# Gated DeltaNet heads 4 to 7: output made channel by token, its norm summed with products with ones

## Chip, cores and metric

The kernel runs on one core of one Trainium2 chip. The time is the device time of one execution in microseconds (us); for the kernel before it is the median of three runs.

## What is computed

One layer of a decoder: RMSNorm of x (1024 tokens of 2048 channels), one projection into three head groups, a gate on each, one output projection, a residual sum and a last RMSNorm. The change touches group B, the gated delta rule: 8 heads, 128 channels for keys and for values. Cut to what matters:

```python
q = l2norm(to_heads(q)) * DN_HEAD_DIM ** -0.5        # l2norm: x * rsqrt(sum(x*x) + EPS)
k = l2norm(to_heads(k)); v = to_heads(v)
...                                                   # per chunk, state S (128 x 128) of a head:
v_new = val_c - kcd_c @ S
o_c = qg_c @ S + ai_c @ v_new                         # qg = q * exp(g_cum), ai = tril(q k^T * decay)
S = S * exp(g_last) + kd_c.T @ v_new
...
o = rmsnorm(o, dn_norm_g) * silu(d_z)                 # o * rsqrt(mean(o*o) + EPS) * g, per token and head
```

The output o is linear in q. So the kernel runs the recurrence with q not normed, and puts the norm of q into that of o: with q not normed, o is scaled by rsqrt(mean(o*o) + 128 * EPS * sum(q*q) + 128 * EPS * EPS).

## The kernel before

All work is in fp32. The large products (projection, memory keys and values, output projection) split each operand into a high and a low fp32r part and add three products (`triple`, L574). The two large projections run as seven products of half-size blocks each (`seven`, L1340). Their weights come from HBM through the `raw` and `kept` tiles and are split by ScalarE (a cast into `rhi`) and VectorE (the rest into `rlo`); the left sides go the same way into `lh` and `ll` or `lm`. `split_to` (L564) is this pair of instructions.

Tokens are worked in two halves `hf` of 512 (HT), each of four tiles of 128 (NT = 4, P = 128). Heads go in pairs `p` of two, and heads 0 to 3 (h < NJ = 4) before heads 4 to 7. For a pair and a half there are two parts:

- `front` (L1230) takes q and k of each head, channel by token: a causal convolution with Silu (`conv`, L978), then `qk` (L1000). `qk` turns k to token by channel with four transposes into one PSUM bank (`to_tokens`, L971), sums its squares by token (`sumsq`, L996: four ScalarE passes, each with a read of its accumulator) and scales it into `kd` (`by_token`, L992: four ScalarE passes with a scale per token). It turns q in the same way, sums its squares into `hs[:, 0]`, forms the products of k with k and with q, and multiplies q by the row of decays exp(g_cum), loaded for all partitions from `ecs[hf]` (L1014, L1035). The tiles q, k, `kd` and `ai` go to HBM (`late_d`, L1240), and the two small columns that are needed later go to `late_hs`.
- `back_of` (L1647) calls `front_late` (L1247), which loads the four tiles into `qT`, `kT`, `kd` and `ai` and copies the small columns back into `hs`; `load_u`, for the inverse of the chunk matrix; `values` (L1261), for v; and `back` (L1268), which makes four steps of the recurrence, `scan_step` (L1170), and then `heads_out` (L1211).

A scan step has four groups of products of 128 by 128 per head. The last, L1199 to L1202, makes the output with q and `ai` as standing operands, so that it comes out token by channel. `S.copy(vs, d0)` (L1209) takes it out of PSUM.

`heads_out` sums the squares of the output by token, forms the factor with a power on POOL (`rsqrt_to`, L559), scales the output by token, and turns it with four transposes to channel by token. For heads 0 to 3 ScalarE scales it by the norm's weights (`col2[:, 8:9]`) and it is stored. For heads 4 to 7 the gate, which lies in `g_d`, is loaded into a tile `E` and one VectorE instruction multiplies by weights and gate (L1227); `head_done` (L1675) stores the result.

**Order of the work.** Nothing is issued while the program is written: every call makes an `Op` in a `Plan`. `issue` (L402) lays all operations on the engines with a price for each (`price`, L193; a VectorE pass of n columns is (n + 151) / 0.96 ns, L223), takes deadlines from a pass backwards (`late`, L342), moves the deadlines named in the table `SHIFT` (L75, operation number and ns) and lays the work once more. Each engine, SyncE's queue of DMA issues included, then runs its operations strictly in that order. TensorE's order is thereby fixed too: groups of small products are laid between the large ones. `FITS` (L41) names the ScalarE functions that need a table of their own.

**Tiles.** `ring["kT"]`, `qT`, `vs`, `kd` and `ai` are two slots each; a new tile in a slot waits for every user of the old one (`Slots`, L475). In the backs `front_late` uses the same two sets of five tiles (`back_sets`, L1635) each time. After the last back the slots hold the queries of group C (`cqs`, L1811). `own_set` is four tiles that the fronts use.

Of the kernel before, what the change touches and what calls it, by code (L numbers as in the profile page):

```python
# [11 lines left out]
F32R = mybir.dt.float32r  # L12
AF = mybir.ActivationFunctionType
# [5 lines left out]
P = 128  # L19
# [18 lines left out]
KP = 4  # L38
ON_ACT = (3,)
NEG = -1.0e30  # L40
FITS = {AF.Exp: 1, AF.Silu: 2, AF.Gelu_apprx_tanh: 3}  # L41

# [21 lines left out]
class Plan:  # L64
# [8 lines left out]
    FETCH = 3500.0  # L73
    TABLE, HOLD = 1300.0, 6000.0
    SHIFT = {  # L75
# [5 lines left out]
    }  # L81

    def __init__(self, nc):
# [340 lines left out]
def kernel(  # L424
# [101 lines left out]
    ring["E"] = Ring("E", 2, [P, HT])  # L526
    ring["tn"] = Ring("tn", 4, [P, HT])
    ring["xr"] = Ring("xr", 3, [P, HT + 3])
    ring["hs"] = Ring("hs", 4, [P, 10, NT])
    jk = C([P, HT], "jk", mybir.dt.bfloat16)  # L530
    gr = C([NT * NH, P], "gr")
    small = Ring("small", 8, [P, 8])
# [8 lines left out]
    def tpb():  # L541
# [9 lines left out]
    G.affine_select(out=ident, in_=ident, compare_op=ALU.not_equal, fill=1.0, base=0,  # L551
                    pattern=[[-1, P]], channel_multiplier=1)
    G.memset(ones, 1.0)
    mhalf = C([P, 8], "mhalf")
    G.memset(mhalf, -0.5)
    with rank(0):
# [443 lines left out]
    def qk(h, hf, tiles, hs, gt, bank):  # L1000

        q, k = tiles[:2]
        kd, ai, vs = map(tok, (*tiles[2:4], ring["tn"]()))
        beta, edk = (scs[hf][:, i] for i in (0, 4))
        (kt,) = to_tokens((k, bank))
        sumsq(hs[:, 1], kt)
        V.tensor_scalar(hs[:, 1], hs[:, 1], EPS, None, op0=ALU.add)
        V.reciprocal(hs[:, 3], hs[:, 1])
        V.scalar_tensor_tensor(hs[:, 2], hs[:, 3], -1.0, beta[:, :, h], op0=ALU.mult, op1=ALU.mult)
        V.tensor_tensor(out=hs[:, 3], in0=hs[:, 2], in1=edk[:, :, h], op=ALU.mult)  # L1010
        by_token(kd, kt, hs[:, 3])
        e = tok(ring["E"]())
        Q.dma_start(e.rearrange("p t c -> p (t c)"), e_d[hf][h])
        Q.dma_start(vs.rearrange("p t c -> p (t c)"), row_of(ecs[hf], h))  # L1014
        by_token(e, e, hs[:, 2])
        (qt,) = to_tokens((q, bank))
        sumsq(hs[:, 0], qt)
        V.tensor_scalar(hs[:, 0], hs[:, 0], P * EPS, P * EPS * EPS, op0=ALU.mult, op1=ALU.add)
        rsqrt_to(hs[:, 4], hs[:, 1])
        V.tensor_tensor(out=hs[:, 4], in0=hs[:, 4], in1=hs[:, 1], op=ALU.mult)  # L1020

        ch, cl = (ring["inv"](F32R).rearrange("p (t s c) -> p t s c", s=2, c=P) for _ in range(2))
        for i, src in enumerate((k, q)):
            split_to(ch[:, :, i], cl[:, :, i], tok(src), V)
        for t2 in range(NT // 2):
            d = bank
            for j in range(2):
                tt = 2 * t2 + j
                triple(d[:, j * 2 * P : (j + 1) * 2 * P], (ch[:, tt, 0], cl[:, tt, 0]), (ch[:, tt], cl[:, tt]),
                       True, True, R.cls)  # L1030
            dv = d.rearrange("p (t s c) -> p t s c", s=2, c=P)
            ts = slice(2 * t2, 2 * t2 + 2)
            V.tensor_tensor(out=gt[:, ts], in0=dv[:, :, 0], in1=e[:, ts], op=ALU.mult)
            V.tensor_tensor(out=ai[:, ts], in0=dv[:, :, 1], in1=e[:, ts], op=ALU.mult)
        V.tensor_tensor(out=q, in0=q, in1=vs.rearrange("p t c -> p (t c)"), op=ALU.mult)  # L1035

    def blocks_out(gt, n):

# [131 lines left out]
    def scan_step(hf, hp, tt, qs, ks, rest, ut):  # L1170

        egl, ngb = scs[hf][:, 3], scs[hf][:, 5]
        sl = slice(tt * P, (tt + 1) * P)
        heads = []
        for i, h in enumerate(hp):
            kd, ai, vs = (t[:, tt] for t in rest[i])
            at = 2 * i if scan_banks[0] is scan_banks[1] else 0
            d = [scan_banks[i][:, (at + k) * P : (at + k + 1) * P] for k in range(2)]
            heads.append((st[h], qs[i][:, sl], ks[i][:, sl], kd, ai, vs, ut[:, i, tt], *d, r3[i], ww[i],
                          egl[:, tt, h : h + 1], ngb[:, tt, h : h + 1]))  # L1180

        first, last = hf == tt == 0, (hf, tt) == (1, NT - 1)
        with rank(1):
            if not first:
                with R.together():
                    for s, q, k, kd, ai, vs, u, d0, d1, r, w, e, n in heads:
                        PE.matmul(d0, k, s, start=True, stop=True)
                for s, q, k, kd, ai, vs, u, d0, d1, r, w, e, n in heads:
                    V.scalar_tensor_tensor(r, d0, n, vs, op0=ALU.mult, op1=ALU.add)
            with R.together():  # L1190
                for s, q, k, kd, ai, vs, u, d0, d1, r, w, e, n in heads:
                    PE.matmul(d1, u, vs if first else r, start=True, stop=True)
            for s, q, k, kd, ai, vs, u, d0, d1, r, w, e, n in heads:
                S.activation(w, d1, AF.Copy, scale=-1.0)
            with R.together():
                if not last:
                    for s, q, k, kd, ai, vs, u, d0, d1, r, w, e, n in heads:
                        PE.matmul(d1, kd, w, start=True, stop=True)
                for s, q, k, kd, ai, vs, u, d0, d1, r, w, e, n in heads:  # L1199
                    if not first:  # L1200
                        PE.matmul(d0, q, s, start=True, stop=False)
                    PE.matmul(d0, ai, w, start=first, stop=True)  # L1202
            for s, q, k, kd, ai, vs, u, d0, d1, r, w, e, n in heads:
                if first:
                    V.tensor_copy(s, d1)
                elif not last:
                    V.scalar_tensor_tensor(s, s, e, d1, op0=ALU.mult, op1=ALU.add)
            for s, q, k, kd, ai, vs, u, d0, d1, r, w, e, n in heads:
                S.copy(vs, d0)  # L1209

    def heads_out(hf, hp, hss, rest):  # L1211
        obs = [vs for kd, ai, vs in rest]

        for hs, ob in zip(hss, obs):
            sumsq(hs[:, 5], ob)
            V.scalar_tensor_tensor(hs[:, 6], hs[:, 5], 1.0 / P, hs[:, 0], op0=ALU.mult, op1=ALU.add)
            rsqrt_to(hs[:, 7], hs[:, 6])
            by_token(ob, ob, hs[:, 7])
        for h, ob, bank in zip(hp, obs, scan_banks):
            (tp,) = to_tokens((ob.rearrange("p t c -> p (t c)"), bank))  # L1220
            if h < NJ:
                S.activation(ob, tp, AF.Copy, scale=col2[:, 8:9])
                Q.dma_start(tok(o_d[hf][h]), ob)
            else:
                e, y = ring["E"](), ob.rearrange("p t c -> p (t c)")
                Q.dma_start(e, g_d[hf][h - NJ])
                V.scalar_tensor_tensor(ob, tp, col2[:, 8:9], tok(e), op0=ALU.mult, op1=ALU.mult)  # L1227
                head_done(h, hf, y)

    def front(p, hf, banks):  # L1230

# [2 lines left out]
        for i, h in enumerate(hp):  # L1234
# [1 line left out]
            conv(1, h, hf, tiles[1])  # L1236
            conv(0, h, hf, tiles[0])
            qk(h, hf, tiles, hs, gt[:, i], banks[i])
            V.tensor_copy(late_hs[:, hf, h], hs[:, 0:5:4])
            for d, t in zip(late_d[hf][h], tiles[:4]):  # L1240
                Q.dma_start(d, t)
        gdr = blocks_out(gt, f"{hf}{p}")
# [4 lines left out]
    def front_late(p, hf):  # L1247

        hp = (2 * p, 2 * p + 1)
        qs, ks, hss, rest = [], [], [], []  # L1250
        for h, tiles in zip(hp, back_sets):
            hss.append(ring["hs"]())
            V.tensor_copy(hss[-1][:, 0:5:4], late_hs[:, hf, h])
            for d, t in zip(late_d[hf][h], tiles):
                Q.dma_start(t, d)
            qs.append(tiles[0])
            ks.append(tiles[1])
            rest.append([tok(t) for t in tiles[2:]])
        return hf, hp, qs, ks, hss, rest

    def values(hf, hp, qs, ks, hss, rest):  # L1261
        for i, h in enumerate(hp):
            v = ring["tn"]()
            conv(2, h, hf, v)
            bank = scan_banks[i]
            by_token(rest[i][2], to_tokens((v, bank))[0], hss[i][:, 4])

    def back(hf, hp, qs, ks, hss, rest, ut):  # L1268
        for tt in range(NT):
            scan_step(hf, hp, tt, qs, ks, rest, ut)  # L1270
        heads_out(hf, hp, hss, rest)


    late_hs = C([P, 2, NH, 2, NT], "lhs")

    def halves(t):
        n = t.shape[1] // 2
# [476 lines left out]
    scan_banks = dnr.bufs[0:2]  # L1754
    hand = dnr.bufs[3]
    wide = acc
    el = over([abh[:, 0:HT], ring["tn"].bufs.pop()])
    for hf in range(2):
        spatial(hf)
# [331 lines left out]
```

## Time and profile before

| | |
|---|---|
| median of 3 runs | 1561.24 us (1560.71 to 1561.47) |
| profiled execution | 1558.44 us |
| its span, first to last instruction | 1556.7 us |
| granted TensorE clock, mean | 0.998 |
| HBM read and written | 336.58 MB, 100.40 MB |
| fronts of heads 4 to 7 | within 600 to 850 us of the span |
| recurrences of heads 4 to 7 | within 965 to 1175 us |

How to read the lines below: an engine is PE (TensorE), PEld (its weight loads), DVE (VectorE), ACT (ScalarE), POOL (GpSimd) or SP (SyncE, which only issues DMA). A group has the form "line engine operation out<-in shape xcount | busy us, mean ns of one | idle time of the engine before them, and what ended it". Since all operations are issued at L420, groups are told apart by tile names, with the buffer number left out: `dn` and `acc` are PSUM banks, `os` is a tile of `own_set`, and a transpose is a product with `ident`, so `dn<-ident,vs` turns a `vs` tile. A product of two full fp32 tiles shows as four records (x112 is 28 products), a transpose or an fp32r product as one. Records of products overlap: their pace is the distance of their starts. A row of a stretch gives start and end, length, busy time and number of instructions by engine, then granted clock, DMA share and GB/s. A row of waits is "who <- for whom: us in total, times, longest".

### The profile page before, as it was taken

The numbers are of one execution on the slowest core, as the hardware profiler recorded it, in microseconds if no ns is written. First come the engines' busy times: TensorE is split into PE (matmuls) and PEld (weight loads), VectorE is DVE, ScalarE is ACT, GpSimd is POOL, SyncE is SP. The second block draws the span as 40 slices with busy tenths as digits, with TensorE's granted clock in tenths as the row PEclk, the third lists the DMA queues.
The fourth block names the chain that finished last, engine by engine and source line by source line (L and its number), as shares of the span: only waits on it lengthen the run. The fifth ranks groups of instructions, "written<-read, shape, count | busy, mean of one in ns | idle before, by whom it ended". The sixth has DMA issues, their size and how long they took to land.

```text
span 1556.7 us, 25174 instructions
## 1 busy us (share of the span) xinstructions
PE 1546.4 (99%) x8725; PEld 1299.2 (83%) x8725; DVE 1250.4 (80%) x1843; ACT 947.8 (61%) x1942; POOL 102.0 (7%) x125
## 2 busy tenths in 40 slices
PE   9999999999999999999999999999999999999997
PEld 8988888888888888888888888888888888888886
DVE  6966974777898946788789975878758999998996
ACT  7833385565874335698885454776557874464554
POOL 0100000100021000010111010010000000000000
PEclk9999999999999999999999999999999999999999
DMA  9999976999879797786797987999958999775984
GB/s 326 308 303 332 310 258 220 308 329 311 297 248 296 239 276 223 265 281 198 260 327 270 326 242 230 310 328 333 346 208 271 314 333 328 268 254 198 342 276 174
DMA packets 348642, 438.68 MB, mean 282 GB/s; under 512 B 78553, under 2 KB 183394, under 8 KB 348514
## 3 DMA queue, kind: packets, MB, share of 16 engines
q1 hardware_dynamic: 346930, 434.37, 85.4%
q0 software_dynamic: 1088, 2.10, 0.5%
q8 instruction: 69, 1.13, 0.3%
q10 hardware_dynamic: 496, 0.61, 0.1%
q14 instruction: 59, 0.48, 0.1%
HBM read 336.58 MB, written 100.40 MB: 281 GB/s over the span
## 4 chain that ended last, share of the span: by engine, by line
PE 95%; DVE 3%; issue 1%; ACT 1%; DMA 0%; POOL 0%; POOLq 0%; SPq 0%; DVEq 0%; ACTq 0%
PE acc L420 60%; PE dn L420 35%; DVE rlo L420 1%; DVE ll L420 0%; DVE tn L420 0%; DVE obs L420 0%; DVE raw L420 0%; DVE inv L420 0%; DMA raw<-in_w_mem_kv_dram 0%; ACT E L420 0%; DVE rs L420 0%; DVE kept L420 0%; DVE xa L420 0%; ACT lh L420 0%; DVE small L420 0%
## 5 line engine op out<-in xcount | busy, mean ns | idle before, releaser
L420 PE MATMUL acc<-lh,rhi 128*128 128x512 f32 x1024 | 395.4, 395 | 0.0
L420 PE MATMUL acc<-lh,rlo 128*128 128x512 f32 x1024 | 384.8, 396 | 0.0
L420 ACT CAST rhi<-raw 128x1024 fp32r<-128x1024 f32 (+1 forms) x145 | 183.3, 1265 | 210.1 <-PE dn L420 106.6
L420 DVE TENSOR_TENSOR rlo<-raw,rhi 128x1024 fp32r<-128x1024 f32 (+1 forms) x145 | 215.5, 1486 | 95.8 <-ACT rhi L420 83.7
L420 PE MATMUL acc<-ll,rhi 128*128 128x512 f32 x688 | 267.1, 395 | 0.1
L420 PEld LDWEIGHTS acc<-lh,rhi 128*128 128x128 f32 x1024 | 192.3, 188 | 37.0 <-ACT qT L420 0.2
L420 PEld LDWEIGHTS acc<-lh,rlo 128*128 128x128 f32 x1024 | 191.6, 188 | 37.0
L420 PEld LDWEIGHTS acc<-ll,rhi 128*128 128x128 f32 x688 | 129.2, 188 | 25.1 <-DVE ll L420 0.6
L420 DVE TENSOR_TENSOR ll<-ll,lh 128x1024 fp32r<-128x1024 f32 x105 | 128.3, 1222 | 11.0 <-ACT lh L420 10.3
L420 PE MATMUL acc<-lm,rhi 128*128 128x512 f32 x336 | 131.6, 394 | 0.0
L420 ACT CAST lh<-ll 128x1024 fp32r<-128x1024 f32 (+1 forms) x107 | 111.5, 1043 | 23.8 <-PE dn L420 9.7
L420 PE MATMUL dn<-lh,rhi 128*128 128x512 f32 x288 | 112.6, 393 | 0.0
L420 PE MATMUL dn<-lh,rlo 128*128 128x512 f32 x288 | 110.8, 394 | 0.0
L420 PE MATMUL dn<-ll,rhi 128*128 128x512 f32 x192 | 75.1, 392 | 0.0
L420 DVE TENSOR_TENSOR rlo<-kept,rhi 128x1024 fp32r<-128x1024 f32 (+1 forms) x38 | 52.7, 1389 | 25.6 <-ACT rhi L420 25.5
L420 PEld LDWEIGHTS acc<-lm,rhi 128*128 128x128 f32 x336 | 63.2, 188 | 12.0
L420 ACT CAST rhi<-kept 128x1024 fp32r<-128x1024 f32 (+1 forms) x38 | 45.3, 1192 | 42.7 <-PE acc L420 25.4
L420 DVE TENSOR_TENSOR raw<-raw,kept 128x1536 f32<-128x1536 f32 (+1 forms) x42 | 64.3, 1532 | 3.2 <-DMA raw<-in_w_in_dram 2.3
L420 POOL TENSOR_TENSOR hs<-hs,mhalf 128x4 f32<-128x4 f32 x32 | 45.8, 1433 | 298.1 <-DVE hs L420 298.1
L420 PEld LDWEIGHTS dn<-lh,rhi 128*128 128x128 f32 x288 | 54.2, 188 | 10.2
L420 PEld LDWEIGHTS dn<-lh,rlo 128*128 128x128 f32 x288 | 54.1, 188 | 10.4
L420 POOL TENSOR_TENSOR small<-small,mhalf 128x1 f32<-128x1 f32 x26 | 19.7, 758 | 634.4 <-DVE small L420 634.4
(500 smaller groups left out, 3460.1 us busy)
## 6 DMA issues: line engine op xcount, KB each, us to landing
raw<-in_w_in_dram SPq DMA_DIRECT2D x168, 256.0 KB
raw<-in_w_in_dram SPq DMA_DIRECT2D x72, 512.0 KB
raw<-in_w_out_dram SPq DMA_DIRECT2D x64, 512.0 KB
ll<-hsd SPq DMA_DIRECT2D x54, 512.0 KB
lm<-hsd SPq DMA_DIRECT2D x26, 512.0 KB
pd<-obs SPq DMA_DIRECT2D x48, 256.0 KB
late<-os SPq DMA_DIRECT2D x44, 256.0 KB
ll<-h0d SPq DMA_DIRECT2D x18, 512.0 KB
```

Of the source, the lines that this page charges most:

```text
L420: o.fn(*o.args, **o.kw)
```

## The change

For heads 4 to 7 the last two products of a scan step have their operands exchanged, so that the output comes out channel by token; it is not turned afterwards. The norm then needs sums over partitions, one for each token: `heads_out` forms (in place of q and k) 128 * EPS * q*q + o*o / 128 + EPS * EPS for each channel and token, splits it, and multiplies it by a matrix of ones, `ones_r`, which puts the sum over all channels into every partition. The factor is the square root of the reciprocal of that sum. q is no longer turned or summed in `qk`, and it is stored without the decay row; `front_late` loads the row into one of two tiles `faded` (from `own_set`) and multiplies there, so that the plain q stays in `qT`. For heads 0 to 3 the old way stands under the name `heads_turned`, with the small columns in `late_hs` and `late_q`. `front_late` takes new tiles from the slots for every pair; the high and low parts of the split are new tiles in the slots of `kd` and `ai`. `Sqrt` becomes a fourth function with a table of its own in `FITS`. The table of deadlines is another one: 30 entries in place of 33, for the operations as they are now numbered.

```diff
-FITS = {AF.Exp: 1, AF.Silu: 2, AF.Gelu_apprx_tanh: 3}
+FITS = {AF.Exp: 1, AF.Silu: 2, AF.Gelu_apprx_tanh: 3, AF.Sqrt: 4}
...
-        410: 8000, 616: -3000, 5881: 8000, 6077: -25600, 6106: 10700, 6120: -9300, 6123: -4300, 6178: 11600,
...
+        5947: -23300, 5980: 8700, 5990: -8000, 5994: -8000, 6011: 11300, 7734: 8000, 8595: -8000, 8727: 23300,
...
+    ones_r = C([P, P], "onesr", F32R)
+    with rank(0):
+        S.copy(ones_r, ones)
...
     def qk(h, hf, tiles, hs, gt, bank):
...
-        Q.dma_start(vs.rearrange("p t c -> p (t c)"), row_of(ecs[hf], h))
+        if h < NJ:
+            Q.dma_start(vs.rearrange("p t c -> p (t c)"), row_of(ecs[hf], h))
         by_token(e, e, hs[:, 2])
-        (qt,) = to_tokens((q, bank))
-        sumsq(hs[:, 0], qt)
-        V.tensor_scalar(hs[:, 0], hs[:, 0], P * EPS, P * EPS * EPS, op0=ALU.mult, op1=ALU.add)
+        if h < NJ:
+            (qt,) = to_tokens((q, bank))
+            sumsq(hs[:, 0], qt)
+            V.tensor_scalar(hs[:, 0], hs[:, 0], P * EPS, P * EPS * EPS, op0=ALU.mult, op1=ALU.add)
...
-        V.tensor_tensor(out=q, in0=q, in1=vs.rearrange("p t c -> p (t c)"), op=ALU.mult)
+        if h < NJ:
+            V.tensor_tensor(out=q, in0=q, in1=vs.rearrange("p t c -> p (t c)"), op=ALU.mult)
...
     def scan_step(hf, hp, tt, qs, ks, rest, ut):
...
-                for s, q, k, kd, ai, vs, u, d0, d1, r, w, e, n in heads:
-                    if not first:
-                        PE.matmul(d0, q, s, start=True, stop=False)
-                    PE.matmul(d0, ai, w, start=first, stop=True)
+                for s, q, k, kd, ai, vs, u, d0, d1, r, w, *_ in heads:
+                    for n, pair in enumerate(((q, s), (ai, w))[first:]):
+                        PE.matmul(d0, *(pair if hp[0] < NJ else reversed(pair)), start=n == 0, stop=n + first == 1)
...
+    def heads_out(hf, hp, raw_q, ks, rest):
+
+        for h, q, k, (kd, ai, vs), bank in zip(hp, raw_q, ks, rest, scan_banks):
+            o, e = vs.rearrange("p t c -> p (t c)"), ring["E"]()
+            S.activation(q, q, AF.Square, scale=math.sqrt(P * EPS))
+            S.activation(k, o, AF.Square, scale=1.0 / math.sqrt(P))
+            V.scalar_tensor_tensor(q, k, EPS * EPS, q, op0=ALU.add, op1=ALU.add)
+            hi, lo = ring["kd"](F32R), ring["ai"](F32R)
+            split_to(hi, lo, q, V)
+            with R.together():
+                PE.matmul(bank, ones_r, hi, start=True, stop=False)
+                PE.matmul(bank, ones_r, lo, start=False, stop=True)
+            V.reciprocal(k, bank)
+            S.activation(k, k, AF.Sqrt)
+            V.tensor_tensor(out=o, in0=o, in1=k, op=ALU.mult)
+            Q.dma_start(e, g_d[hf][h - NJ])
+            V.scalar_tensor_tensor(o, o, col2[:, 8:9], e, op0=ALU.mult, op1=ALU.mult)
+            head_done(h, hf, o)
...
     def front_late(p, hf):
...
+        for h in hp:
+            tiles = [ring[tag]() for tag in ("qT", "kT", "kd", "ai", "vs")]
             for d, t in zip(late_d[hf][h], tiles):
                 Q.dma_start(t, d)
-            qs.append(tiles[0])
+            q = tiles[0]
+            if h >= NJ:
+                q = faded()
+                Q.dma_start(q, row_of(ecs[hf], h))
+                V.tensor_tensor(out=q, in0=q, in1=tiles[0], op=ALU.mult)
+            raw_q.append(tiles[0])
+            qs.append(q)
...
+    faded = over(own_set[0:2])
```

More of the change, by code (lines that the diff above doesn't have):

```diff
@@ L528 @@
     ring["xr"] = Ring("xr", 3, [P, HT + 3])
-    ring["hs"] = Ring("hs", 4, [P, 10, NT])
+    ring["hs"] = Ring("hs", 4, [P, 5, NT])
     jk = C([P, HT], "jk", mybir.dt.bfloat16)
@@ L1002, in qk @@
         q, k = tiles[:2]
-        kd, ai, vs = map(tok, (*tiles[2:4], ring["tn"]()))
+        kd, ai = map(tok, tiles[2:4])
+        vs = tok(ring["tn"]()) if h < NJ else None
         beta, edk = (scs[hf][:, i] for i in (0, 4))
@@ L1209, in scan_step, with heads_turned @@
                 S.copy(vs, d0)
[L1211 to L1218, printed above, removed]
+    def heads_turned(hf, hp, rest):
+        obs, hss = [vs for kd, ai, vs in rest], [ring["hs"]() for _ in hp]
+        for h, hs, ob in zip(hp, hss, obs):
+            sumsq(hs[:, 1], ob)
+            V.scalar_tensor_tensor(hs[:, 2], hs[:, 1], 1.0 / P, late_q[:, hf, h], op0=ALU.mult, op1=ALU.add)
+            rsqrt_to(hs[:, 3], hs[:, 2])
+            by_token(ob, ob, hs[:, 3])
@@ L1219, in heads_out @@
         for h, ob, bank in zip(hp, obs, scan_banks):
             (tp,) = to_tokens((ob.rearrange("p t c -> p (t c)"), bank))
[L1221 to L1228, printed above, removed]
+            S.activation(ob, tp, AF.Copy, scale=col2[:, 8:9])
@@ new lines, in heads_turned @@
+            Q.dma_start(tok(o_d[hf][h]), ob)
+    def heads_out(hf, hp, raw_q, ks, rest):
[15 more added lines that the diff above has]
+            head_done(h, hf, o)
@@ L1238, in front @@
             qk(h, hf, tiles, hs, gt[:, i], banks[i])
-            V.tensor_copy(late_hs[:, hf, h], hs[:, 0:5:4])
+            V.tensor_copy(late_hs[:, hf, h], hs[:, 4])
+            if h < NJ:
+                V.tensor_copy(late_q[:, hf, h], hs[:, 0])
             for d, t in zip(late_d[hf][h], tiles[:4]):
@@ L1249, in front_late, with values @@
         hp = (2 * p, 2 * p + 1)
[L1250 to L1253, printed above, removed]
+        qs, ks, raw_q, rest = [], [], [], []
+        for h in hp:
+            tiles = [ring[tag]() for tag in ("qT", "kT", "kd", "ai", "vs")]
             for d, t in zip(late_d[hf][h], tiles):
                 Q.dma_start(t, d)
-            qs.append(tiles[0])
+            q = tiles[0]
[5 more added lines that the diff above has]
+            qs.append(q)
             ks.append(tiles[1])
             rest.append([tok(t) for t in tiles[2:]])
-        return hf, hp, qs, ks, hss, rest
-    def values(hf, hp, qs, ks, hss, rest):
+        return hf, hp, qs, ks, raw_q, rest
+    def values(hf, hp, qs, ks, raw_q, rest):
         for i, h in enumerate(hp):
@@ L1265, in values, with back @@
             bank = scan_banks[i]
-            by_token(rest[i][2], to_tokens((v, bank))[0], hss[i][:, 4])
-    def back(hf, hp, qs, ks, hss, rest, ut):
+            by_token(rest[i][2], to_tokens((v, bank))[0], late_hs[:, hf, h])
+    def back(hf, hp, qs, ks, raw_q, rest, ut):
         for tt in range(NT):
             scan_step(hf, hp, tt, qs, ks, rest, ut)
-        heads_out(hf, hp, hss, rest)
-    late_hs = C([P, 2, NH, 2, NT], "lhs")
+        if hp[0] < NJ:
+            heads_turned(hf, hp, rest)
+        else:
+            heads_out(hf, hp, raw_q, ks, rest)
+    late_hs, late_q = C([P, 2, NH, NT], "lhs"), C([P, 2, NJ, NT], "lhq")
     def halves(t):
```

7 rows, old and new, of the table SHIFT are left out of this document.

## Prediction

> **What bounds the kernel now.** I read the page first: busy time by engine, then the chain that ended last.
>
> ```profile
> span 1556.7 us, 25174 instructions
> ...
> PE 1546.4 (99%) x8725; PEld 1299.2 (83%) x8725; DVE 1250.4 (80%) x1843; ACT 947.8 (61%) x1942; POOL 102.0 (7%) x125
> ...
> PE 95%; DVE 3%; issue 1%; ACT 1%; DMA 0%; POOL 0%; POOLq 0%; SPq 0%; DVEq 0%; ACTq 0%
> ```
>
> TensorE is busy 99% of the span and is 95% of the chain. A busy PE row can hide stalls, so the next view was the list of waits, for TensorE alone; these two rows are all it has:
>
> ```profile
> PE acc L420 <- POOL ones L420: 1.2, 1, 1.2
> PE dn L420 <- ACT lh L420: 0.2, 1, 0.2
> ```
>
> TensorE waits 1.4 us in 1556.7. So the time is the number of TensorE instructions times the pace of each, and every other engine matters only if it makes TensorE wait. The pace of the large products stands in the chain in order of time, and that of a transpose group in the timeline of TensorE:
>
> ```profile
> 855.26 23.58 PE acc L420 x104
> ```
>
> ```profile
> 1016.87 0.39 PE L420 MATMUL acc<-lh,rhi 128*128 128x512 f32 x1
> 1017.10 0.60 PE L420 MATMUL dn<-ident,tn 128*128 128x128 f32 x4
> 1017.45 0.71 PE L420 MATMUL acc<-lh,rhi 128*128 128x512 f32 x2
> 1018.00 0.60 PE L420 MATMUL dn<-ident,vs 128*128 128x128 f32 x4
> ```
>
> 104 products of 512 columns take 23.58 us, 0.227 us each (the 0.39 us of a row is one product's latency, which overlaps the next). From 1016.87 to 1018.00 lie three such products and one group of four transposes: 1.13 - 3 x 0.227 = 0.45 us for the group. A group of four transposes costs TensorE as much as two products of 512 columns.
>
> **The change, part by part.** *TensorE.* For heads 4 to 7 and both halves of the sequence, eight cases, the change removes the group that turns q in `qk` and the group that turns the output in `heads_out`. The rows by group, the first in the stretch 600 to 850 us, where the fronts of heads 4 to 7 run, the other three in 1000 to 1175 us, where their recurrences run:
>
> ```profile
> L420 PE MATMUL dn<-ident,os 128*128 128x128 f32 x64 | 9.6, 272 | 0.0
> ```
>
> ```profile
> L420 PE MATMUL dn<-steps,ai 128*128 128x128 f32 x56 | 10.7, 275 | 0.0
> L420 PE MATMUL dn<-states,qT 128*128 128x128 f32 x52 | 10.0, 275 | 0.0
> ...
> L420 PE MATMUL dn<-ident,vs 128*128 128x128 f32 x32 | 4.6, 272 | 0.0
> ```
>
> The 64 `os` records are 16 groups, of which the eight of q go (those of k stay); the 32 `vs` records are the eight output groups, and all go. Removed: 16 x 0.45 = 7.2 us. Added: two products of 512 columns with ones per case, 16 x 0.227 = 3.6 us. The two output products of each scan step only swap which operand stands still; all are 128 by 128 either way and both rows show 275 ns, so that is 0. Net on TensorE: 7.2 - 3.6 = 3.6 us less, one transpose group's worth per case.
>
> *VectorE, where the recurrences run.* The busy time by stretch, from the first recurrence step of heads 4 and 5 to past the last of heads 6 and 7, and as a comparison a stretch of the output projection:
>
> ```profile
> core 0: us, PE busy (x) PEld busy (x) DVE busy (x) ACT busy (x) POOL busy (x), PEclk, DMA share, GB/s
> 965.00:1010.00 45.00, 45.00 (x309) 38.59 (x308) 36.17 (x52) 31.61 (x64) 3.93 (x5) 1.00 1.01 305
> 1010.00:1055.00 45.00, 45.00 (x252) 38.68 (x251) 33.58 (x59) 35.66 (x90) 7.88 (x6) 1.00 1.02 332
> 1055.00:1095.00 40.00, 40.00 (x233) 34.86 (x231) 32.48 (x50) 26.16 (x67) 2.83 (x2) 1.00 0.98 330
> 1095.00:1135.00 40.00, 40.00 (x223) 34.50 (x222) 28.34 (x43) 24.95 (x65) 2.01 (x2) 1.00 0.87 308
> 1135.00:1175.00 40.00, 40.00 (x186) 33.38 (x186) 25.46 (x28) 18.35 (x26) 0.00 (x0) 1.00 0.71 245
> sum 210.00, PE 210.00 PEld 180.02 DVE 156.03 ACT 136.73 POOL 16.66; mean PE 42.00 PEld 36.00 DVE 31.21 ACT 27.35 POOL 3.33
> ```
>
> ```profile
> 1280.00:1400.00 120.00, 119.81 (x527) 98.61 (x527) 116.73 (x132) 63.85 (x83) 0.00 (x0) 1.00 0.82 285
> ```
>
> The durations, from the VectorE groups by shape and, for the last row, the rows of tile `sc`:
>
> ```profile
> L420 DVE TENSOR_TENSOR os<-os,tn 128x512 f32<-128x512 f32 x11 | 7.6, 688 | 6.8 <-PE dn L420 6.8
> L420 DVE SCALAR_TENSOR_TENSOR vs<-dn,col,E 128x512 f32<-128x512 f32 x8 | 5.9, 747 | 1.3 <-PE dn L420 1.1
> ...
> L420 DVE RECIPROCAL hs<-hs 128x4 f32<-128x4 f32 x16 | 2.7, 170 | 0.0
> ...
> L420 DVE COPY hs<-lhs 128x8 f32<-128x8 f32 x16 | 2.6, 164 | 0.0
> ...
> L420 DVE SCALAR_TENSOR_TENSOR hs<-hs 128x4 f32<-128x4 f32 x16 | 2.6, 160 | 5.0 <-ACT jk L420 4.9
> ```
>
> ```profile
> L420 DVE RECIPROCAL sc<-sc x2: 295/324/352, 160.8 to 161.1; 128x32 f32<-128x32 f32 x2
> ```
>
> Each case adds here the product of q with its decay row, moved from the front (0.69), the sum of squares (0.75), the low part of the split (0.69), a reciprocal of 128x512 and the product with it (0.69); the last scaling was there before. No row shows a reciprocal of 512 columns. The lower end is a plain pass, 0.69 us. From 4 to 32 columns the reciprocal grows by 154 ns, 5.5 ns a column: 0.17 + 508 x 0.0055 = 2.96 us; with the slower of the two records (352) it is 6.5 ns and 3.47 us, the upper end. I take 2.96, since it rests on the same operation. Per case 5.78 us, for eight 46.2; gone are eight copies of `hs` (0.16 each) and eight small sums (0.16): 2.6. VectorE goes from 156.0 to 199.6 of 210 us, 95%. It stays below the 116.73 of 120 us (97%) of the other stretch, in which TensorE has no row of waiting for it. I cost this at nothing, with VectorE's 54 idle us as cover; if the cover is gone, TensorE waits for `rlo` or `ll` behind it.
>
> By the Trainium skill, page "VectorE: DVE Perf Modes", the walkthrough of the 8-slice pipeline, the reciprocal is an iterative divide with a repeat count of 8; read as 8 cycles a column at the 0.96 GHz of VectorE, an estimate from that page, 512 columns take 4.3 us. The trace's 5.5 ns is some five cycles, not eight, so I keep the row.
>
> *ScalarE.* Rows of the same stretch, 965 to 1175 us:
>
> ```profile
> L420 ACT ACTIVATE vs<-vs,hs 128x128 f32<-128x128 f32 x32 | 10.4, 391 | 2.2 <-POOL hs L420 2.2
> L420 ACT ACTIVATE jk<-vs 128x128 bf16<-128x128 f32 x32 | 9.9, 310 | 0.6
> L420 ACT ACTIVATE obs<-obs 128x512 f32<-128x512 f32 x16 | 9.9, 637 | 4.8 <-DVE obs L420 4.8
> L420 ACT ACT_TABLE_LOAD x7 | 9.0, 1283 | 0.1
> ...
> L420 ACT ACTIVATION_READ_ACCUMULATOR jk<-vs 128x1 f32 x32 | 6.1, 190 | 0.0
> ```
>
> The sums and scalings by token go: 10.4 + 9.9 + 6.1 = 26.4 us. Two squares, a cast and a square root of 512 columns come, 8 x 4 x 0.64 = 20.5, and the square root has a table of its own: between none and two loads more per case, 0 to 20.5 us; I take all, since Silu and Gelu stand between the cases. ScalarE: 136.7 to at most 151.3 of 210. Covered. In the fronts it only loses work. The copy of ones at the start is one 128x128 pass, at most 0.39 us if nothing hides it.
>
> *SyncE and DMA.* Eight loads of a decay row leave the fronts and come back here:
>
> ```profile
> tn<-ecd SPq DMA_DIRECT2D x16, 256.0 KB
> ```
>
> At the 332 GB/s of the fullest stretch, 0.79 us each, 6.3 us: the DMA share goes from 193.8 of 210 us (stretch lengths times shares) to 200.1. The loads of the next pair's q, k, kd and ai now wait in SyncE's queue until the norm has let go of those tiles, where they waited for the recurrence alone; weight loads stand behind them.
>
> *POOL* loses eight powers; nobody on the chain waits for them. *The table* lays every engine's order anew. It can win at most the 1.4 us of waits; what it can lose is in the cases below.
>
> The sum: the profiled execution took 1558.44 us around its span of 1556.7, so 1554.8 for one like it; the median of the runs, 1561.24, lies 2.8 above it, and 1561.24 - 3.6 = **1557.6**. The measurement of this kernel can tell about 0.2% (3.1 us) from no change: faster is below 1558.1, slower above 1564.4. The forecast clears that by little.
>
> **The rivals.** *Late VectorE work eats the gain.* The order is laid out beforehand, and the planner prices the reciprocal like any pass, (512 + 151) / 0.96 = 691 ns, 2.27 us under the row's 2.96. VectorE takes its work in order, so an `rlo` behind a reciprocal comes up to 2.27 us later than planned, 18 us over eight. If a quarter reaches TensorE, 4.5 us: 1562.1. For it: 95% load. Against it: `rlo` has several buffers, and 97% did no harm.
>
> *Slower: SyncE stands still at the handover between pairs.* k is held until its product with the reciprocal is done: square 0.64, sum 0.75, split 0.64 and 0.69, two products 0.45, reciprocal 2.96, table and root 1.92, 0.69 more are 8.7 us after the last step, and two reciprocals make it 4.5 us later than planned. With three handovers, SyncE issues no weights for 13.6 us, and the first four stretches leave DMA only 170 - 165.4 = 4.6 us to catch up, less than the row loads take.
>
> ```profile
> SPq L420 <- DVE vs L420: 9.4, 7, 2.9
> ```
>
> For it: SyncE does already wait for VectorE here, up to 2.9 us at a time. Against it: loads stand some buffers ahead. It decides where half of the 13.6 us reaches TensorE; all of it gives 1561.24 - 3.6 + 13.6 = 1571.2, two handovers 1566.7. The end of the last pair is not at risk:
>
> ```profile
> L420 PE MATMUL dn<-states,qT x112: 270/275/275, 622.4 to 1129.0; 128*128 128x128 f32 x112
> ...
> L420 ACT COPY kT<-acc x2: 587/588/588, 1171.3 to 1172.6; 128x512 f32<-128x512 f32 x2
> ```
>
> its scan ends near 1129 and the next user of those tiles comes at 1171, 42 us against 25: three handovers of 4.5 us, the 8.7 us of k and 3.0 for the second head's reciprocal.
>
> *VectorE becomes the bound.* At 97% it could carry 204.3 of 210 us; with a reciprocal of R us the load is 176.0 + 8R, so this decides from R = 3.54, just above the upper end of the rows, and costs 8 us per us: at R = 4, 3.7 us, and the gain is gone: 1561.3. By the Trainium skill's page "VectorE: DVE Perf Modes", read as above, R would be 4.3 and the time 1563.7, an estimate.
>
> That the transposes stay is no case: the code for heads 4 to 7 has none left.
>
> **How the numbers follow.** The gain arrives whole or nearly: 0.46, 1557.6. Late VectorE work: 0.30, 1558 to 1564. Handover: 0.18. VectorE bound: 0.06, half of it the same, half slower. Faster 0.46, same 0.33, slower 0.21. The likeliest case's own range is 1556.2 (the 1.4 us of waits gone too) to 1558.1. The whole range, 1556.0 to 1567.0, takes in the second case and the handover up to two of three.
>
> **What would show it.** Right: 8725 - 64 + 16 = 8677 products on PE; 56 `ident,os` and 32 `ident,vs`; 16 products with ones 0.227 us apart from their neighbours; eight reciprocals near 3 us; PE waits still under 2 us; a span near 1553.1. Wrong: PE rows waiting for VectorE's `rlo` or `ll` between 965 and 1215 (late work), for DMA of `raw` or `kept` with SyncE waiting for `kT` or `kd` (handover), or VectorE above 97% there.

## The result, and the profile after

The kernel after takes 1578.49 us (median of four runs, 1577.0 to 1579.07); the kernel before, run beside it, 1560.97. The ratio is 1.0111, 95% interval 1.0095 to 1.0127: slower by 17.5 us. The profiled execution took 1577.0 us around a span of 1575.3, 18.6 more than before's span.

From the page of after, the span, the busy time by engine, and the chain that ended last:

```profile
span 1575.3 us, 25008 instructions
...
PE 1547.6 (98%) x8677; PEld 1296.8 (82%) x8677; DVE 1285.4 (82%) x1851; ACT 948.1 (60%) x1823; POOL 91.9 (6%) x117
...
PE 94%; DVE 2%; DMA 1%; issue 1%; ACT 1%; SPq 0%; POOL 0%; POOLq 0%; DVEq 0%; ACTq 0%
```

TensorE has the 8677 instructions that were counted, and the chain still reads as if nothing had happened: 94% in place of 95%. The list of TensorE's waits, which had two rows before, shows it:

```profile
PE dn L419 <- ACT xb L419: 4.5, 1, 4.5
PE acc L419 <- DVE obs L419: 4.0, 2, 2.8
PE acc L419 <- DVE ll L419: 3.0, 2, 1.8
PE acc L419 <- ACT kT L419: 2.5, 1, 2.5
PE dn L419 <- ACT vs L419: 1.8, 2, 1.2
PE acc L419 <- POOL ones L419: 1.2, 1, 1.2
PE dn L419 <- DVE os L419: 0.3, 1, 0.3
PE dn L419 <- DMA kept<-in_mem_dram: 0.3, 1, 0.3
PE dn L419 <- ACT rhi L419: 0.2, 1, 0.2
```

The nine rows sum to 17.8 us where before had 1.4. They are twelve waits, and the long ones are for VectorE, or for ScalarE behind VectorE. The busy time by stretch, as in the prediction, shows where:

```profile
965.00:1010.00 45.00, 45.00 (x250) 38.20 (x248) 41.62 (x60) 29.71 (x56) 2.22 (x3) 1.00 1.00 302
1010.00:1055.00 45.00, 41.30 (x223) 35.07 (x223) 41.92 (x61) 35.29 (x61) 1.48 (x2) 1.00 0.93 297
1055.00:1095.00 40.00, 37.09 (x211) 31.62 (x210) 36.17 (x50) 21.25 (x43) 0.00 (x0) 1.00 0.93 304
1095.00:1135.00 40.00, 35.41 (x176) 29.60 (x175) 36.27 (x43) 22.23 (x39) 0.00 (x0) 0.96 0.87 295
1135.00:1175.00 40.00, 40.00 (x201) 33.91 (x200) 23.72 (x31) 22.86 (x36) 0.00 (x0) 1.00 0.68 234
1175.00:1215.00 40.00, 35.49 (x166) 29.49 (x166) 35.29 (x45) 24.85 (x48) 0.00 (x0) 0.96 0.69 233
```

TensorE (the second number) is no longer full in four of the six stretches, and in two of them its clock falls to 0.96. VectorE (the fourth) is busier, but nowhere full: 41.92 of 45 us, 93%, at most. The groups by shape:

```profile
L419 DVE RECIPROCAL kT<-dn 128x512 f32<-128x512 f32 x8 | 26.4, 3331 | 1.8 <-PE dn L419 1.8
...
L419 PE MATMUL dn<-ident,os 128*128 128x128 f32 x56 | 8.4, 272 | 0.3 <-DVE os L419 0.3
...
L419 PE MATMUL dn<-ident,vs 128*128 128x128 f32 x32 | 4.9, 274 | 0.0
...
L419 PE MATMUL dn<-kd,onesr 128*128 128x512 f32 x8 | 3.1, 394 | 0.0
L419 PE MATMUL dn<-ai,onesr 128*128 128x512 f32 x8 | 3.1, 392 | 0.0
```

A reciprocal of 512 columns takes 3.33 us; the planner priced it at 0.69. Three of the four pairs of heads have their two back to back. The timeline of VectorE at the first pair, then that of TensorE:

```profile
1004.13 1.22 DVE L419 TENSOR_TENSOR rlo<-raw,rhi 128x1024 fp32r<-128x1024 f32 x1
1005.27 6.56 DVE L419 RECIPROCAL kT<-dn 128x512 f32<-128x512 f32 x2
1011.75 0.63 DVE L419 TENSOR_TENSOR obs<-acc,yu 128x512 f32<-128x512 f32 x1
1012.30 1.21 DVE L419 TENSOR_TENSOR ll<-ll,lh 128x1024 fp32r<-128x1024 f32 x1
```

```profile
1009.23 0.84 PE L419 MATMUL acc<-lh,rlo 128*128 128x512 f32 x3
1012.53 0.47 PE L419 MATMUL acc<-lh,rhi 128*128 128x512 f32 x1 [2.46 <-ACT kT L419]
```

The pass `obs<-acc,yu` empties a PSUM bank of the large products. It has nothing to do with heads 4 to 7, but it stands behind the two reciprocals, and TensorE waits 2.46 us to write that bank again. The profile names ScalarE's `kT` as the releaser, since that ended last before 1012.53; `obs` ended at 1011.75 + 0.63 = 1012.38, 0.15 us ahead of the product. At the third pair, where the profile does name `obs`, the distance is the same 0.15 us.

At the last pair another chain ends in the longest wait. VectorE, ScalarE and TensorE there:

```profile
1181.56 6.56 DVE L419 RECIPROCAL kT<-dn 128x512 f32<-128x512 f32 x2
...
1189.71 1.28 DVE L419 TENSOR_TENSOR vs<-vs,kT 128x512 f32<-128x512 f32 x2
```

```profile
1190.48 1.19 ACT L419 COPY kT<-acc 128x512 f32<-128x512 f32 x2 [1.70 <-DVE vs L419]
1191.57 0.62 ACT L419 CAST xb<-kT 128x512 fp32r<-128x512 f32 x1
```

```profile
1192.24 0.84 PE L419 MATMUL dn<-gt,xb 128*128 128x256 f32 x4 [4.51 <-ACT xb L419]
```

The queries of group C take over the `kT` slots, which the norm holds until `vs<-vs,kT`; that product comes after the two reciprocals, and the queries, their split `xb` and TensorE's product come after it.

### The profile page after: what moved, and what is told of

Its sections match the earlier page's. It is cut to its first block, busy times and chain, and to the rows that moved or that the text cites. A ratio compares the mean times of both kernels' runs of the same rounds, so it can differ in the third digit from the quotient of the medians.

```text
span 1575.3 us, 25008 instructions
## 1 busy us (share of the span) xinstructions
PE 1547.6 (98%) x8677; PEld 1296.8 (82%) x8677; DVE 1285.4 (82%) x1851; ACT 948.1 (60%) x1823; POOL 91.9 (6%) x117
## 4 chain that ended last, share of the span: by engine, by line
PE 94%; DVE 2%; DMA 1%; issue 1%; ACT 1%; SPq 0%; POOL 0%; POOLq 0%; DVEq 0%; ACTq 0%
PE acc L419 59%; PE dn L419 35%; DVE kT L419 1%; DMA ll<-hTd 0%; DMA kept<-in_mem_dram 0%; DMA qT<-late 0%; DVE vs L419 0%; DVE ll L419 0%; ACT vs L419 0%; SPq L419 0%; DVE obs L419 0%; DVE lm L419 0%; DVE rlo L419 0%; DVE inv L419 0%; ACT jk L419 0%
## 5 line engine op out<-in xcount | busy, mean ns | idle before, releaser
L419 DVE TENSOR_TENSOR ll<-ll,lh 128x1024 fp32r<-128x1024 f32 x105 | 128.7, 1225 | 21.6 <-ACT lh L419 21.4
L419 PEld LDWEIGHTS dn<-lh,rlo 128*128 128x128 f32 x288 | 54.1, 188 | 10.6
L419 DVE TENSOR_TENSOR lm<-lm,lh 128x1024 fp32r<-128x1024 f32 x42 | 51.6, 1229 | 6.3 <-ACT lh L419 6.2
```

The source lines that it names most:

```text
L419: o.fn(*o.args, **o.kw)
```

## Experiments

My theory at this point was: **the reciprocals' unplanned length on VectorE** (3.33 - 0.69 = 2.64 us, eight times 21 us) reaches TensorE through whatever stands behind them in VectorE's order. The rivals were the new order of all work, the handover of tiles and SyncE's queue, and the added work as such. In what follows each time stands beside that of the kernel before in the same comparison.

**The reciprocal's length alone taken away** (all engines keep after's order; the norm is then not inverted, here and in each kernel with copies below):

```diff
-            V.reciprocal(k, bank)
+            V.tensor_copy(k, bank)
```

> The changed kernel with the reciprocal of 128x512 replaced by a plain VectorE copy from the same bank (so the norm of heads 4 to 7 is not inverted: that part of the computation is left out). The planner prices both alike, 691 ns, so every engine's order is the same as in the changed kernel, operation for operation. Theory 1, late VectorE work: the eight reciprocals take 3.33 us each where the order was laid out for 0.69, and TensorE waits behind them; without their 21 us the time is near the 1557.6 us that the count of products gives (1556 to 1560), and the TensorE waits between 1005 and 1195 us of the span go. Rival, the handover: q, k, kd and ai are still let go by the norm alone, so at least half of the loss stays, 1568 or more. Rival, the new table and order: the order is the same, so the time stays at 1577 to 1579.

Measured: 1558.58 against 1559.51, ratio 0.9994 (0.9985 to 1.0003). TensorE's waits in it:

```profile
PE acc L419 <- POOL ones L419: 1.2, 1, 1.2
PE dn L419 <- DMA kept<-in_mem_dram: 0.5, 1, 0.5
PE dn L419 <- DVE os L419: 0.3, 1, 0.3
PE acc L419 <- DVE ll L419: 0.2, 1, 0.2
```

Some 18 us are gone with the length, and so are the long waits. Handover, transfers, order and the other added work are all still in this kernel, so none of them alone is the cause.

**The price mended in the planner:**

```diff
+            if name == "reciprocal":
+                o.cost = 130.0 + 6.25 * n
```

> The changed kernel with one line more in the planner's prices: a reciprocal of n columns costs 130 + 6.25 n ns, 3.33 us for 512, as measured. The same operations, the same table of deadlines, but laid out in another order. Theory 1 in the form 'not the work but the wrong price': 1558 to 1565, since other passes are then laid ahead of the reciprocals and TensorE's products later. Rival, VectorE is simply too full between 965 and 1215 us: 1570 or more. A table that was fitted to the other order may cost some us in either case.

Measured: 1580.96 against 1559.51, 1.0134 (1.0119 to 1.0149), no better than after, where 1558 to 1565 was expected if the price alone was at fault. The long waits in one place are gone; the two largest rows are now these:

```profile
PE acc L421 <- DVE rlo L421: 4.2, 3, 1.9
PE acc L421 <- ACT oh L421: 1.9, 1, 1.9
```

The rest is spread over the whole span. A new price shifts every operation, and the 30 entries of the table move deadlines that were chosen in another order. So this run alone does not tell a missing price from missing room.

**No reciprocal: factor as exp(-0.5 ln(sum))** on ScalarE, laid out anew (`FITS` names `Ln` in place of `Sqrt`):

```diff
-            V.reciprocal(k, bank)
-            S.activation(k, k, AF.Sqrt)
+            S.activation(k, bank, AF.Ln)
+            S.activation(k, k, AF.Exp, scale=-0.5)
```

> The changed kernel with the factor formed on ScalarE alone: exp(-0.5 ln(sum)) in place of reciprocal and square root, one operation for one, so the numbering and the table stay; VectorE has eight passes of 3.33 us fewer, ScalarE eight of 0.6 more. Theory 1: 1556 to 1561. Rival, the handover or the new order in itself: little better than 1578.

Measured: 1566.57 against 1559.51, 1.0041 (1.0027 to 1.0055), more than the 1556 to 1561 expected. Most of the loss is gone, not all: this order is also a new one under an old table.

**The true price and the reciprocal in four pieces**, the price line as above and the table kept on the same operations:

```diff
-            V.reciprocal(k, bank)
+            for i in range(4):
+                V.reciprocal(k[:, i * 128 : (i + 1) * 128], bank[:, i * 128 : (i + 1) * 128])
```

> The changed kernel with each reciprocal in four pieces of 128 columns, each priced at its true 0.93 us; the table is applied to the same operations as before. The same VectorE work in all (24 instructions more, about 3 us), but nothing has to wait longer than 0.93 us for a piece. Theory 1, a long block that cannot be interrupted: 1558 to 1564, better than the whole reciprocal with its true price. Rival, VectorE too full: no better than that one, 1570 or more.

Measured: 1578.75 against 1559.51, 1.0124 (1.0109 to 1.0139). Other work could now be laid between the pieces, and nothing clear of noise was gained on the whole reciprocal at its true price. That speaks against the idea that the size of one block is what hurts, as far as one order can show it.

**All tables emptied**, to take that disturbance out (`key[i] += 0.0 * t` in place of `key[i] += t`): the kernel before, the kernel after, after with the copy, and after with the true price.

> The kernel before with its table of deadlines emptied: the planner's own deadlines alone. It says what a table is worth, so that the runs with another price can be read: their waits of TensorE lay all over the span, at 64, 867, 903, 949, 1297 and 1317 us too, which no reciprocal explains. If the table does no more than trim, 1561 to 1566; if the order leans on it, 1570 or more.

> The changed kernel with its table emptied, the reciprocal priced at 691 ns as in the change. Theory 'late reciprocals': above the same with a copy in the reciprocal's place (the next run) by 15 to 22 us, as with the table. Theory 'it is the new table': no slower than the changed kernel with its table.

> The kernel of the run before with a VectorE copy in place of the reciprocal (the norm is not inverted, that part is left out), every engine's order the same as there. It is the floor for this comparison without tables: within 4 us of the kernel before with its table emptied.

> The changed kernel with its table emptied and the reciprocal priced at 130 + 6.25 n ns. Without tables only price and work differ from the two runs before. Theory 'wrong price': within 5 us of the run with the copy, since the order then knows of the 3.33 us. Theory 'VectorE has no room': within 5 us of the run with the wrong price.

Measured against 1559.87: 1563.01 for before (1.0020, 1.0011 to 1.0029), 1588.09 for after (1.0182, 1.0167 to 1.0197), 1566.65 with the copy (1.0042, 1.0027 to 1.0057), 1576.2 with the true price (1.0104, 1.0087 to 1.0120). Two things follow. The table of before is worth 3.1 us, so a lost table can't cost 17; nor is after's own table at fault, since after without it is slower still (1588.09 against 1578.49). And without tables the length of the reciprocals costs 1588.09 - 1566.65 = 21.4 us again; a planner that knows it gets 11.9 of them back, and 9.5 stay, which is between what the two theories expected.

**Reciprocal off VectorE, order kept.** As the third experiment, but Ln is issued on ScalarE at the reciprocal's place in the program, priced and laid as the reciprocal and the root were:

```diff
-            V.reciprocal(k, bank)
-            S.activation(k, k, AF.Sqrt)
+            R.add("dve", "reciprocal", lambda *a: nc.scalar.activation(*a, AF.Ln), (k, bank), {})
+            R.add("act", "activation", lambda o, i, _: nc.scalar.activation(o, i, AF.Exp, scale=-0.5), (k, k, AF.Sqrt), {})
```

> The changed kernel with the factor formed on ScalarE as exp(-0.5 ln(sum)), but in the very order of the changed kernel: the logarithm is issued where the reciprocal stood, the exponential where the square root stood, and the planner sees no difference. VectorE loses eight passes of 3.33 us, ScalarE gains eight of 0.63 us and a few table loads. Theory 1: as with the copy, 1557 to 1560, 0 to 2 us under the kernel before, since the first run with logarithm and exponential (1566.6) lost its time to an order that the table was not made for. Rival, the ScalarE way is itself too slow: 1564 or more.

**The reciprocals alone added to before**, ahead of the last scaling of heads 4 to 7, unknown to the planner, order otherwise the same (their output is overwritten):

```diff
+                    nc.vector.reciprocal(o, src)
                     return nc.vector.scalar_tensor_tensor(o, *a, **kw)
```

> The kernel before, with its own table and order, and nothing added but eight reciprocals of 128x512 on VectorE from the same bank and into the same tile, one right ahead of the last scaling of each of heads 4 to 7; the planner does not know of them. Theory 1, a pass of 3.33 us that the order does not know of makes TensorE wait wherever it stands: 10 to 25 us over the kernel before, less than in the change if VectorE has more idle time there. Rival, the reciprocals hurt only with the rest of the change (operands exchanged, tiles held longer, VectorE's other added passes): under 4 us.

Measured against 1559.25: 1559.79 (1.0002, 0.9993 to 1.0011) and 1587.89 (1.0182, 1.0168 to 1.0196). The first is the change's whole computation in after's order, and its loss is gone. The second has nothing of the change but eight reciprocals, in the well laid order of before, and loses 28.6 us, more than the 10 to 25 expected. Its group of reciprocals, and the longest of TensorE's waits:

```profile
L1228 DVE RECIPROCAL vs<-dn 128x512 f32<-128x512 f32 x8 | 26.8, 3353 | 0.8 <-PE dn L420 0.8
```

```profile
PE dn L420 <- DVE vs L1229: 11.7, 5, 2.8
PE dn L420 <- DVE xb L420: 5.3, 1, 5.3
PE dn L420 <- DVE small L420: 3.0, 1, 3.0
```

Here the reciprocal itself holds back the scaling that empties the bank (`vs`, L1229).

**How the loss grows.** Does a single reciprocal fit into some slack and only a pair of them hurt, or does every one count? In after's order four of the eight stay and four become copies, once the first of each pair of heads (`V.reciprocal if h % 2 == 0 else V.tensor_copy`), once both of the first pair of each half (`if h < NJ + 2`).

> The kernel after in its own order on every engine, but the reciprocal stays only for the first head of each pair (four of eight); for the second head VectorE copies the sum at that place, so the norm of heads 5 and 7 is not inverted. No two reciprocals stand back to back any more. Theory A (every unplanned microsecond of VectorE in this stretch reaches TensorE): half of the 20 us between the kernel with eight reciprocals (1578.5) and the one with eight copies (1558.6) is lost: 1568 to 1570. Theory B (the order has some slack, which one reciprocal's 2.6 us fits into and two in a row do not): clearly less than half, 1559 to 1564.

> As g1, but the reciprocal stays for both heads of the first pair of each half (heads 4 and 5, four of eight, back to back) and heads 6 and 7 have the copy, so that their norm is not inverted. Theory A (every unplanned microsecond counts alike): the same time as g1, 1568 to 1570. Theory B (slack that a single one fits into): about half of the 20 us, 1567 to 1571, and some 5 us or more above g1.

Measured against 1558.80: 1567.95 (1.0058, 1.0045 to 1.0070) and 1569.01 (1.0065, 1.0052 to 1.0079). The longest waits of the first, then those of the second:

```profile
PE dn L419 <- ACT xb L419: 1.9, 1, 1.9
PE acc L419 <- DVE ll L419: 1.8, 1, 1.8
PE acc L419 <- DVE obs L419: 1.4, 2, 1.2
```

```profile
PE acc L419 <- DVE obs L419: 4.0, 2, 2.8
PE acc L419 <- ACT kT L419: 2.5, 1, 2.5
PE acc L419 <- DVE ll L419: 2.0, 2, 1.8
```

The second has after's rows for `obs` and `kT`, to a tenth, at the pairs that kept the reciprocals; the 4.5 us for `xb`, at a pair with copies, is gone. Set side by side, with the unplanned VectorE time, what it costs over the same order without it, and how much longer TensorE waits in the profiled executions (all rows of the lists of waits):

| kernel | unplanned, us | cost, us | TensorE waits longer, us | over |
|---|---|---|---|---|
| first of each pair | 4 x 2.64 = 10.6 | 9.15 + 0.93 = 10.1 | 7.4 - 2.2 = 5.2 | the copies in after's order |
| first pair of each half | 10.6 | 10.21 + 0.93 = 11.1 | 10.5 - 2.2 = 8.3 | the same |
| after | 8 x 2.64 = 21.2 | 17.5 + 0.93 = 18.4 | 17.8 - 2.2 = 15.6 | the same |
| after, no table | 21.2 | 21.4 | 23.2 - 7.9 = 15.3 | the copies, no table |
| before with reciprocals | 26.8 | 28.6 | 22.5 - 1.4 = 21.1 | before |

(9.15, 10.21 and 17.5 are the distances to the kernel before; the copies are 0.93 below it.) Each unplanned microsecond of VectorE in this stretch costs 0.87 to 1.07 us of time, in three orders, singly or in pairs; by the intervals a cost is uncertain by some 2 to 3 us. As waits of TensorE, though, only 0.5 to 0.8 us of each microsecond shows. So the order does have some slack: with the first of each pair alone, half of the 10.6 us ended in no wait. The time did not gain by it, since TensorE also runs at half clock after some waits (last section): two stretches of 3.4 us in the first of these kernels (from 1109.39 and 1184.49) and one in the second (from 1110.57), each at a granted clock of 0.50 and so 1.7 us of work lost.

## Why the prediction was wrong

**What held.** The counts (8677, 56, 32 and 16 records), products with ones 394 and 392 ns long like the others, and ScalarE, with 31 table loads for 23 before, within the zero to sixteen more that were allowed for:

```profile
L419 ACT ACT_TABLE_LOAD x31 | 39.8, 1283 | 2.8 <-issue 2.2
```

VectorE's load too. The kernel with copies, from 965 to 1175 us:

```profile
965.00:1175.00 210.00, 209.91 (x1118) 178.77 (x1117) 174.77 (x254) 139.62 (x245) 3.72 (x5) 1.00 0.92 302
```

VectorE's 174.8 and the 21.2 us that the reciprocals are longer make 196 of 210, where 199.6 was predicted.

**The reciprocal** was mis-sized by little: 2.96 us taken, 3.47 as the upper end, 3.33 measured. From 4 columns to 512 that is (3331 - 170) / 508 = 6.2 ns a column, nearer to the slower of the two records of 32 columns (6.5) than to their mean (5.5). The eight cycles a column that I read out of the page "VectorE: DVE Perf Modes" of the Trainium skill, the walkthrough of the 8-slice pipeline, 4.3 us as an estimate, the trace does not bear out.

**The step that failed** is "I cost this at nothing, with VectorE's 54 idle us as cover", and with it, in the rival that was right in kind, "if a quarter reaches TensorE". Of 8 x 2.64 = 21.2 us unplanned, 15.6 became waits of TensorE, three quarters and not one; two stretches at half clock, for which the prediction has no term, took 3.4 us more, and 18.4 us were lost in all. At the prediction's own 2.27 us a cost of one microsecond for each would have been 18.2 us, and 1557.6 + 18.2 = 1575.8. The row that I set against it, 116.73 of 120 us busy with no wait of TensorE, says that VectorE can be 97% busy if the order was laid for it. It says nothing on work that comes late. The idle time of VectorE lies where it waits for its own inputs; that little of it can be used by work that is late already is what the table above shows, and why no more of it can was not tried. What is shown as the cause is the length of the reciprocals. That a planner which knows the length would avoid the loss is shown in part only: it won 11.9 of 21.4 us without tables and nothing in the two runs with a table that was made for another order.

**SyncE at the handover** did not decide: TensorE's only wait for a transfer in after is 0.3 us at the start, and the kernel with the copies has the same handovers at 1558.6. But "the end of the last pair is not at risk" was wrong, for a reason that before's trace could have told. The 42 us were counted from the end of the scan; the norm of the last pair is laid much later. The rows of before for the last scaling:

```profile
L420 DVE SCALAR_TENSOR_TENSOR vs<-dn,col,E x8: 736/748/753, 1014.8 to 1170.1; 128x512 f32<-128x512 f32 x8
```

The last one starts at 1170.1, just ahead of the queries' copy at 1171.3. In before it held no `kT` slot; in after it does, and this is the 4.5 us wait for `xb`. Without the reciprocals' length it does not show: the copies' kernel has no row for `xb`.

**TensorE's 3.6 us** were mis-sized too, and do not show in the time even where the reciprocals are harmless: -0.93 us with copies (the interval, -2.3 to +0.5 us, excludes 3.6), +0.5 with Ln and Exp. The page of the kernel with copies:

```profile
PE 1545.2 (99%) x8677; PEld 1295.8 (83%) x8677; DVE 1265.4 (81%) x1851; ACT 948.7 (61%) x1823; POOL 94.5 (6%) x117
```

TensorE is busy 1.2 us less than in before (1546.4), and 0.8 of them go into more waits (2.2 against 1.4). One part of the miss stands in the prediction's own rows: the four transposes start at 1017.10 and the next product at 1017.45, so that the group takes 0.35 us. The 0.45 also took in the two products behind it, 0.55 us where two at the usual pace take 0.45. Summed over the two traces from start to start, the transposes take 5.4 us less in the kernel with copies, 0.36 us a group in before, and the products with ones take 3.7 us more, which leaves 1.7 us. Why other products take 0.5 us more has no cause that a run shows. Without tables the copies' kernel is 3.6 us above before (1566.65 against 1563.01), and there TensorE waits 3.0 us longer (7.9 against 4.9). How much of the loss a fitting order could save stays open. No version here is measurably faster than before.

## What to carry to other kernels

When an order is fixed ahead, price every new kind of instruction from a row of its own before it goes in: what one instruction takes longer than the planner thinks can arrive nearly whole in the time, as waits of the bounding engine and as a lower clock after them, however idle its own engine is on average, if the bounding engine has no waits left. Read VectorE's and ScalarE's queues for what stands behind the new instruction, above all passes that empty PSUM banks or let go of tiles, rather than their share of busy time. To find such a cause, keep the order and change only the duration.

## What the runs showed of the hardware

After some of its longer waits TensorE runs at half clock for 3.4 us. The stretch around the third pair's waits and the two slow stretches of after (granted clock third from the end, TensorE's busy time the second number):

```profile
1110.90:1114.30 3.40, 0.52 (x2) 0.24 (x2) 3.40 (x6) 1.57 (x2) 0.00 (x0) 0.99 0.94 308
1114.40:1117.70 3.30, 3.30 (x8) 2.62 (x9) 3.30 (x6) 1.77 (x3) 0.00 (x0) 0.51 0.99 354
1192.90:1196.20 3.30, 3.30 (x13) 3.06 (x13) 3.30 (x7) 1.38 (x3) 0.00 (x0) 0.51 0.98 279
```

In the slow stretches products of 512 columns are 0.427 us apart instead of 0.227; two of some 3.4 us at half clock are 3.4 us of work lost, on top of the 15.6 us that after waits longer than the kernel with the copies (the sum, 19.0, against 17.5 between their spans). The Trainium skill, page "TensorE: Matmul & The Clock Gate", Part 1, has the gate look at activity in free-running windows of 3413 ns and fall back to half rate after an idle one; the length agrees. A wholly idle window was not needed here, though. In the kernel with the first reciprocal of each pair, TensorE waited only 1.90 us, and this followed:

```profile
1181.00:1184.40 3.40, 1.50 (x10) 1.00 (x9) 3.40 (x6) 2.64 (x4) 0.00 (x0) 1.00 0.32 119
1184.60:1187.80 3.20, 3.20 (x11) 2.73 (x11) 3.20 (x6) 2.06 (x3) 0.00 (x0) 0.50 1.00 262
```

With 1.50 busy us in 3.4, less than half, the next stretch ran at 0.50. The wait of 2.46 us that ended at 1012.53 in after had no such stretch behind it. Counted back from the slow stretch at 1114.25 in steps of 3.413 us, it lies in two windows, from 1008.43 and from 1011.84, in which TensorE was busy 1.64 and 2.72 us. No sharp limit shows: in the kernel with four pieces a stretch with 1.75 busy us, from 1191.97 to 1195.38, was followed by one at 0.50.
